# Second MLP product of a two-layer trunk: 12 of 16 pairs of k tiles computed with seven block products, their input sums made in the first product's stage

## The chip, the cores and the metric

The kernel runs on one core of a Trainium2 chip. A core has TensorE (PE, matmuls, whose weight loads the profile lists as PEld), VectorE (DVE), ScalarE (ACT), GpSimd (POOL) and SyncE (SP, which here only issues DMAs), each with its own queue of instructions, worked off in order. The metric is the device time of one execution, in microseconds. The kernel before took 3173.66 us (median of three runs, 3168.63 to 3181.02).

## What is computed

A trunk of two layers over 1024 tokens of width 1024. Layer 0 mixes tokens with two recurrent head groups, layer 1 with chunked attention. Every layer then has an MLP of inner width 4096 and a gated embedding. The reference, cut to what matters here:

```python
for i in range(DEPTH):
    ...
    x = x + mix
    hf = rmsnorm(x, norm_ffn_g[i])
    x = x + jnp.square(jax.nn.relu(hf @ mlp_w1[i])) @ mlp_w2[i]
    x = x + rmsnorm(p[i] @ ple_w_proj[i], ple_norm_g[i]) * jax.nn.sigmoid(x @ ple_w_gate[i])
return x
```

`mlp_w1[i]` is 1024 x 4096 and `mlp_w2[i]` 4096 x 1024, all in fp32.

## The kernel before

**Precision.** A product in fp32 is made of three matmuls in the format fp32r: each operand is split into a high part (a cast by ScalarE) and a low part (the operand minus the high part, by VectorE), and high x high, high x low and low x high are summed in PSUM (`mm3`). A matmul takes a 128x128 block of weights and 128x512 of activations (features on partitions, tokens along the row). `split` (L1264 to L1270) is the cast, L1269, and the subtraction, L1270.

**Stages.** `tail(i)` runs after the mixer of layer i, in one pass each for: the output projection (adds `mix` to the residual), the first MLP product, the second one, and the gate with the per-layer embedding. The residual has 8 tiles of 128 features; each is kept in two halves of 512 tokens (`self.xh`, `self.xh2`), in DRAM during the first product.

**First product, as seven block products.** The 32 output tiles are taken as 16 pairs, p = 0 to 15, and tokens in two halves, so that each round p is a 2x2 block problem over 8 input tiles in 4 pairs. In place of eight products of blocks, seven (numbered m, in the order 1, 2, 5, 6, 7, 3, 4) are made from sums and differences of blocks, each of 4 x 3 = 12 matmuls. The sums on the activation side (`cmb`) were made in the output projection. Those on the weight side, of the raw weights loaded by `raws(p)`, are made a round ahead by `prepare(p, m)` (L1337, L1341 and a split). A product lands in one of eight PSUM banks; the sums of products that give the four blocks of the output are made by VectorE in `plus` (L1371), into a ring of 8 quarter tiles (`scr`). `hidden` (L1374) applies relu and square on ScalarE and stores the block to DRAM (`self.hd`) on ScalarE's DMA queue, 256 KB each.

**Row statistics.** The norm's 1/rms of each token isn't known when the first product starts and is applied after it (squared, since relu and square come between). `squares(n)` loads residual tile n, squares it on ScalarE and adds it on VectorE (L1307 to L1315), one tile after each of the rounds p = 0 to 7, in the ring's tiles. After p = 8, `row_stats` sums over features with matmuls against ones, takes the inverse root in ten small vector operations in a row (L284 to L289, from the bank's copy at L373), and `to_rows` transposes the result with 8 small matmuls (L190) and copies it to `rs`; L1444 squares it.

**Second product.** `mlp2(g)` for g = 0 to 7 takes 4 of the 32 k tiles at a time. Their hidden tiles are loaded (L1397), multiplied by `rs` (L1401) and split during the group before; the weights come in 512 KB pieces (L1273) and are split, one piece ahead. For each of the 8 output tiles and both token halves 12 matmuls go into a bank, and VectorE adds the bank to the residual (L1470). After the last group the residual is split for the gate.

**What sets the order.** `tail` is a generator, run beside others that have work in the same stretch; within an engine the instructions stand in the order that a planner gives them from the dependencies and the program's order. Tiles come from pools: the pool of tag "a" has six places of 128 x 2 x 1024, in which weights and raw data take turns, so a tile's first write waits for the readers of the tile that had the place before. PSUM banks go round in the same way. All loads go through SyncE's queue in order, the hidden stores through ScalarE's.

Of the kernel before, what the change touches and what calls it, by code (L numbers as in the profile page):

```python
# [17 lines left out]
P = 128  # L18
# [8 lines left out]
PLAN_ROWS = 2  # L27

# [79 lines left out]
class Trunk:  # L108
# [56 lines left out]
    def mm(self, out, lhsT, rhs, start, stop):  # L165
# [9 lines left out]
        return self.begin(self.nc.tensor.matmul(out, lhsT, rhs, start=start, stop=stop))  # L175
# [129 lines left out]
    def mm3(self, ps, wh, wl, xh, xl, first, last):  # L305
        nc, steps = self.nc, self.steps
        ins = self.mm(ps, wh, xh, start=first, stop=False)
# [5 lines left out]
        self.mm(ps, wh, xl, start=False, stop=False)  # L313
        self.mm(ps, wl, xh, start=False, stop=last)
# [886 lines left out]
    def tail(self, i, xsrc):  # L1201
# [13 lines left out]
        with ExitStack() as es:  # L1215
# [46 lines left out]
            self.hd = [self.dr.tile([P, T], F32, tag=f"hd{k}", name="hd") for k in range(32)]  # L1262
# [106 lines left out]
            def plus(t, u):  # L1369
                r = scr()  # L1370
                V.tensor_tensor(r, t, u, op=ALU.add)  # L1371
                return r

            def hidden(t, k, hf):  # L1374
                A.activation(t, t, AF.Relu)
                A.activation(t, t, AF.Square)
                nc.scalar.dma_start(out=self.hd[k][:, hs[hf]], in_=t)

            H = [pB[0:4], None]

            w2 = {}

            rawb = []

            def raw_b():
                if not rawb:
                    rawb.extend(halves(place(F32)))
                return rawb.pop(0)

            def load_w2(n):  # L1390
                w2[n] = weights(a["w2"][i, n // 4, n % 4], raw_b(), place(F32R))

            hraw = {}

            def fetch_hidden(n, raw):
                hraw[n] = raw
                nc.sync.dma_start(out=raw, in_=self.hd[n])  # L1397

            def load_hidden(n):
                raw = hraw.pop(n)  # L1400
                V.tensor_tensor(raw, raw, rs, op=ALU.mult)  # L1401
                split(H[n // 4 % 2][n % 4], raw)

# [3 lines left out]
            for p in range(16):  # L1407
                k = 2 * p
# [589 lines left out]
```

## Time and profile before

| | |
|---|---|
| runs before | 3168.63, 3173.66, 3181.02 us |
| profiled execution, span from first to last instruction | 3174.0 us |
| mean granted clock of TensorE | 0.973 |
| busy: TensorE / VectorE / ScalarE / GpSimd | 96% / 64% / 44% / 17% |
| HBM read, written | 232.16 MB, 74.45 MB |
| tail of layer 0, by the chain of waits | 951.59 to about 1681 us |
| tail of layer 1 | 2370.99 us to the end |

A line of a timeline gives start, length, engine, line and operation, the tiles written and read, and in brackets how long the engine had been idle and what ended that. A line of groups gives the count, the busy time and the mean of one in ns, and the idle time ahead of such instructions. A line of the chain of waits gives start, length and what ran; "dps" is a PSUM bank. A matmul record is longer than the distance between two of them, since they overlap; the same holds for the vector and scalar records.

### The profile page before, as it was taken

What the parts mean: (1) busy time and instruction counts of PE and PEld (TensorE: products, weight loads), DVE (VectorE), ACT (ScalarE), POOL (GpSimd) and SP (SyncE); (2) the same over time, 40 slices, a digit from 0 to 9 for tenths busy, and PEclk for the clock granted to TensorE, in tenths of its full rate; (3) what the DMA queues carried; (4) which work ended last, traced back from release to release, by engine and by line L of the source; (5) the groups of instructions that cost most, each with busy time, mean ns of one, the idle gap of its engine ahead of it and who ended that gap; (6) DMA issues with size and microseconds to landing.
All of it is one profiled execution on the core that took longest, in us unless ns stands there. A gap on an engine that the chain in (4) does not pass through costs nothing.

```text
span 3174.0 us, 46034 instructions
## 1 busy us (share of the span) xinstructions
PE 3057.5 (96%) x17576; PEld 2523.9 (80%) x17576; DVE 2018.1 (64%) x4020; ACT 1387.8 (44%) x2640; POOL 536.1 (17%) x978
## 2 busy tenths in 40 slices
PE   7999999999999999999999989999999999999999
PEld 5777777777778888888887888888788888888887
DVE  6546666567849666655556576776769666655552
ACT  4323433333427554311223577777757555312221
POOL 6524443444500000000005111110200000000002
PEclk8989999999999999999999999999999999999999
DMA  3212112112345333522213100110255332522213
GB/s 128 77 48 64 50 43 85 54 57 64 126 153 209 136 120 112 190 93 100 99 54 129 58 32 33 47 39 16 76 197 205 136 120 107 199 93 93 107 47 106
DMA packets 144716, 309.60 MB, mean 98 GB/s; under 512 B 40944, under 2 KB 43120, under 8 KB 144496
## 3 DMA queue, kind: packets, MB, share of 16 engines
q1 hardware_dynamic: 126064, 273.10, 25.1%
q10 hardware_dynamic: 18432, 33.56, 2.7%
q8 instruction: 138, 2.26, 0.3%
q14 instruction: 82, 0.67, 0.1%
HBM read 232.16 MB, written 74.45 MB: 97 GB/s over the span
## 4 chain that ended last, share of the span: by engine, by line
PE 79%; DVE 10%; ACT 4%; DMA 4%; issue 2%; POOL 1%; SPq 0%; DVEq 0%; POOLq 0%; ACTq 0%
PE dps L175 67%; PE ch L175 2%; PE po L175 1%; PE pm L175 1%; PE iz L175 1%; PE tp L175 1%; DVE ptile L348 1%; PE pt L190 1%; DVE f L1056 1%; DMA wraw<-in_w_out 1%; PE sn L175 1%; DMA wraw<-in_w_qkv 1%; DVE wlo L302 1%; DVE pb L1838 1%; POOL subt L413 1%
## 5 line engine op out<-in xcount | busy, mean ns | idle before, releaser
L175 PE MATMUL dps<-r,act 128*128 128x512 f32 x3528 | 824.4, 392 | 0.0
L175 PEld LDWEIGHTS dps<-r,act 128*128 128x128 f32 x3528 | 662.2, 188 | 145.6
L175 PE MATMUL dps<-xg,whi 128*128 128x512 f32 x1280 | 437.9, 423 | 16.2 <-ACT xg L350 7.1
L175 PE MATMUL dps<-late,act 128*128 128x512 f32 x1536 | 352.9, 391 | 0.0
L175 PEld LDWEIGHTS dps<-late,act 128*128 128x128 f32 x1536 | 288.5, 188 | 63.1
L1495 POOL TENSOR_TENSOR pn<-pn,prs 128x512 f32<-128x512 f32 x32 | 47.1, 1475 | 1621.3 <-ACT prs L384 1527.3
L175 PE MATMUL dps<-wq,act 128*128 128x384 f32 x1536 | 304.8, 343 | 8.0 <-DVE vs L1747 4.2
L175 PEld LDWEIGHTS dps<-xg,whi 128*128 128x128 f32 x1280 | 237.2, 197 | 67.0 <-ACT xg L350 7.1
L175 PEld LDWEIGHTS dps<-wq,act 128*128 128x128 f32 x1536 | 264.5, 190 | 12.6 <-DVE vs L1747 7.0
L175 PE MATMUL dps<-xg,wlo 128*128 128x512 f32 x640 | 260.4, 408 | 2.0 <-DVE wlo L302 2.0
L1371 DVE TENSOR_TENSOR late<-late,dps 128x512 f32<-128x512 f32 x224 | 152.7, 684 | 152.4 <-PE dps L175 120.3
L1470 DVE TENSOR_TENSOR xw<-xw,dps 128x512 f32<-128x512 f32 x192 | 131.5, 685 | 154.6 <-PE dps L175 151.4
L1269 ACT CAST act<-act 128x1024 fp32r<-128x1024 f32 (+1 forms) x99 | 94.7, 963 | 282.9 <-DMA act<-in_w 119.4
L1269 ACT CAST act<-late 128x512 fp32r<-128x512 f32 x210 | 124.5, 618 | 139.5 <-PE dps L175 120.2
L1270 DVE TENSOR_TENSOR act<-late,act 128x512 fp32r<-128x512 f32 x210 | 139.7, 686 | 25.9 <-ACT act L1269 25.7
L175 PEld LDWEIGHTS dps<-xg,wlo 128*128 128x128 f32 x640 | 125.5, 196 | 33.2 <-DVE wlo L302 4.1
L301 ACT CAST whi<-wraw 128x1024 fp32r<-128x1024 f32 x78 | 81.7, 1048 | 152.7 <-PE dps L175 91.4
L175 PE MATMUL dps<-xw,act 128*128 128x512 f32 x576 | 138.9, 392 | 0.0
L175 PEld LDWEIGHTS dps<-xw,act 128*128 128x128 f32 x576 | 108.1, 188 | 24.1
L1270 DVE TENSOR_TENSOR act<-act 128x1024 fp32r<-128x1024 f32 (+1 forms) x99 | 109.9, 1114 | 18.3 <-ACT act L1269 17.2
L175 PE MATMUL po<-ptile,vs 128*128 128x256 f32 (+1 forms) x576 | 103.3, 293 | 17.5 <-DVE ptile L348 8.5
L302 DVE TENSOR_TENSOR wlo<-wraw,whi 128x1024 fp32r<-128x1024 f32 x78 | 99.3, 1274 | 27.5 <-ACT whi L301 27.1
(472 smaller groups left out, 5284.9 us busy)
## 6 DMA issues: line engine op xcount, KB each, us to landing
act<-in_w SPq DMA_DIRECT2D x68, 512.0 KB
hd<-late ACTq DMA_DIRECT2D x128, 256.0 KB
late<-in_w SPq DMA_DIRECT2D x60, 512.0 KB
wraw<-in_w_in SPq DMA_DIRECT2D x56, 512.0 KB
act<-hd SPq DMA_DIRECT2D x56, 512.0 KB
wraw<-in_w_out SPq DMA_DIRECT2D x21, 512.0 KB
wraw<-in_w_qkv SPq DMA_DIRECT2D x21, 512.0 KB
pn<-pnd SPq DMA_DIRECT2D x32, 256.0 KB
```

Source lines behind the costliest of these rows:

```text
L175: return self.begin(self.nc.tensor.matmul(out, lhsT, rhs, start=start, stop=stop))
L190: return self.begin(self.nc.tensor.transpose(out, in_, ident))
L301: nc.scalar.copy(hi, raw)
L302: nc.vector.tensor_tensor(lo, raw, hi.bitcast(F32), op=ALU.subtract)
L348: nc.vector.tensor_tensor(dst[:, 1, sl], src, dst[:, 0, sl].bitcast(F32), op=ALU.subtract)
L413: E.tensor_tensor(o, X[:, 0:i, i:i + 1].broadcast_to((NP, i, n)), Bq[:, i:i + 1, i + 1:16].broadcast_to((NP, i, n)), op=ALU.mult)
L1056: V.scalar_tensor_tensor(y, raws[j][:, i:i + HB], cw(i), y, op0=ALU.mult, op1=ALU.add)
L1269: A.copy(hi, s)
L1270: V.tensor_tensor(lo, s, hi.bitcast(F32), op=ALU.subtract)
L1371: V.tensor_tensor(r, t, u, op=ALU.add)
L1470: V.tensor_tensor(x[n][:, sl], x[n][:, sl], ps, op=ALU.add)
L1495: G.tensor_tensor(pn, pn, prs[:, sl], op=ALU.mult)
```

## The change

- The first 8 hidden tiles (the pairs p = 0 to 3, `PLAIN` = 4) are still stored as they are and multiplied plainly, in two groups of 4 k tiles: `plain(0)` at the start of the second product's stage and `plain(1)` at its end.
- The other 12 pairs are multiplied as 2x2 blocks with seven block products, four pairs at a time. In round n (0 to 11) the products of pairs n to n+3 (cyclic) are made for output pair n % 4; each round replaces one pair of the four, so that after three turns every output pair has seen all 12. A round is 7 products of 12 matmuls, in the order 1, 5, 6, 2, 7, 3, 4.
- Products 1, 6, 7, 4 add up in one PSUM bank without being cleared, 5 and 3 in another, 2 has its own. After each product VectorE adds the bank's present content to one block of the residual (`add_to`), and the next product of the chain goes on adding to it.
- The seven activation-side blocks are made in the first product's rounds p = 4 to 15 and stored to DRAM (`self.hb`, 7 x 256 KB a round in place of 4 x 256 KB): four scalings by `rs` and four differences on VectorE. For that, `rs` is needed from p = 4 on, so `squares` goes through three tiles after each of p = 0, 1, 2, with the single buffer "pl", and `row_stats` comes after p = 2.
- In the second product `block` loads and splits one stored block per product, and `raws2(n)` loads 4 x 256 KB of weights a round, of which `prepare2` makes and splits the weight side. `w2` is laid out anew by the host.
- `plus` writes in place where it can.

The diff, cut to its core:

```diff
+PLAIN = 4
+NB = 16 - PLAIN
...
-        return self.begin(self.nc.tensor.matmul(out, lhsT, rhs, start=start, stop=stop))
+        return self.begin(self.nc.tensor.matmul(out, lhsT, rhs, start=start, stop=stop, skip_group_check=again))
...
-            self.hd = [self.dr.tile([P, T], F32, tag=f"hd{k}", name="hd") for k in range(32)]
+            self.hd = [self.dr.tile([P, T], F32, tag=f"hd{k}", name="hd") for k in range(2 * PLAIN)]
+            self.hb = {p: self.dr.tile([P, 7, HB], F32, tag=f"hb{p}", name="hb") for p in range(PLAIN, 16)}
...
             def squares(n):
 
+                both = self.pre.tile([P, 2, HB], F32, tag="pl", name="xq")
                 for hf, src in ((0, self.xh[n]), (1, self.xh2[n])):
-                    t = scr()
+                    t = both[:, hf]
                     nc.sync.dma_start(out=t, in_=src)
                     if n:
...
-            def plus(t, u):
-                r = scr()
+            def plus(t, u, out=None):
+                r = out if out is not None else scr()
                 V.tensor_tensor(r, t, u, op=ALU.add)
                 return r
 
-            def hidden(t, k, hf):
+            def hidden(t, p, r, hf):
+
                 A.activation(t, t, AF.Relu)
                 A.activation(t, t, AF.Square)
-                nc.scalar.dma_start(out=self.hd[k][:, hs[hf]], in_=t)
-
...
+                if p < PLAIN:
+                    nc.scalar.dma_start(out=self.hd[2 * p + r][:, hs[hf]], in_=t)
+                else:
+                    V.tensor_tensor(t, t, rs[:, hs[hf]], op=ALU.mult)
+                    if (r, hf) != (0, 1):
+                        store(p, {(0, 0): 1, (1, 0): 2, (1, 1): 3}[r, hf], t)
+                return t
+
+            def store(p, m, t):
+                nc.scalar.dma_start(out=self.hb[p][:, m - 1], in_=t)
+
+            def differ(p, m, u, v, out=None):
+                t = out if out is not None else scr()
+                V.tensor_tensor(t, u, v, op=ALU.subtract)
+                store(p, m, t)
+                return t
...
+            def load_w2(g, u):
+                t, raw = place(F32R), self.pre.tile([P, 2, HB], F32, tag="pl", name="w2")
+                for j in range(2):
+                    nc.sync.dma_start(out=raw[:, j], in_=a["w2"][i, 2 * g + j, u])
+                split(t, raw.rearrange("p j c -> p (j c)"))
+                w2[g, u] = t[:, 0], t[:, 1]
...
+            def load_hidden(t, raw):
                 V.tensor_tensor(raw, raw, rs, op=ALU.mult)
-                split(H[n // 4 % 2][n % 4], raw)
+                split(t, raw)
...
+            def raws2(n):
+                t = place(F32)
+                for j in range(4):
+                    nc.sync.dma_start(out=t.rearrange("p q c -> p (q c)")[:, j * HB:j * HB + HB],
+                                      in_=a["w2"][i, PLAIN + (n + j) % NB, n % 4])
+                v = t.rearrange("p q c -> p (q c)").rearrange("p (j b c) -> p b j c", b=4, c=P)
+                prep2[n] = [v[:, b] for b in range(4)], {}
+
+            prep2, free2 = {}, []
+
+            def prepare2(n, m):
+
+                (a11, a12, a21, a22), d = prep2[n]
+                if not free2:
+                    free2.extend(parts(place(F32R)))
+                d[m] = free2.pop(0)
+                if m == 5:
+                    V.tensor_tensor(a21, a21, a22, op=ALU.add)
+                o, u, v = {1: (a11, None, None), 2: (a12, None, None), 5: (a21, None, None), 6: (a11, a21, a11),
+                           7: (a21, a22, a11), 3: (a12, a12, a11), 4: (a22, None, None)}[m]
+                if u is not None:
+                    V.tensor_tensor(o, u, v, op=ALU.subtract)
+                split(d[m], o)
+
+            def block(q, m):
+
+                raw = braw()
+                nc.sync.dma_start(out=raw, in_=self.hb[PLAIN + q % NB][:, m - 1])
+                split(areas[m][q % 4], raw)
...
                 if p < 15:
                     raws(p + 1)
                 else:
-                    for j in range(4):
-                        fetch_hidden(j, lt[2 + j // 2][:, j % 2])
-                    load_w2(0)
+                    load_w2(0, 0)
...
-                        hidden(plus(p1, ps), k, 0)
+                        c11 = hidden(plus(p1, ps), p, 0, 0)
                     elif m == 5:
                         p5 = ps
                     elif m == 6:
-                        u2 = plus(p1, ps)
+                        u2 = plus(p1, ps, p1)
                         u4 = plus(u2, p5)
                     elif m == 7:
-                        u3 = plus(u2, ps)
-                        hidden(plus(u3, p5), k + 1, 1)
+                        u3 = plus(u2, ps, u2)
+                        c22 = hidden(plus(u3, p5), p, 1, 1)
                     elif m == 3:
-                        hidden(plus(u4, ps), k, 1)
+                        c12 = hidden(plus(u4, ps, u4), p, 0, 1)
+                        if p >= PLAIN:
+                            differ(p, 7, c22, c12)
+                            t1 = differ(p, 5, c12, c11, c12)
+                            t2 = differ(p, 6, c22, t1)
                     else:
-                        hidden(plus(u3, ps), k + 1, 0)
+                        c21 = hidden(plus(u3, ps, u3), p, 1, 0)
+                        if p >= PLAIN:
+                            differ(p, 4, c21, t2)
                     if p < 15:
                         prepare(p + 1, prep_order[q])
+                    elif q == 1:
+                        hid = [fetch_hidden(0, k, h0[k], lt[2 + k // 2][:, k % 2]) for k in range(4)]
                     elif 2 <= q < 6:
-                        load_hidden(q - 2)
+                        load_hidden(*hid[q - 2])
                     yield 0
-                if p < NK:
-                    squares(p)
-                if p == NK:
+                if p < 3:
+                    for n in range(3 * p, min(3 * p + 3, NK)):
+                        squares(n)
+                if p == 2:
                     self.row_stats(accs, col)
...
+            areas[6], areas[2], areas[7], areas[3], areas[4] = pq[8:12], pq[12:16], cmb[4], pq[0:4], pq[4:8]
+            braw = ring([self.accp.tile([P, HB], F32, tag=f"acc{q}", name="braw") for q in range(2)] + quarters(place(F32)))
+            areas[1], areas[5] = [[c for q in qs for c in parts(place(F32R, True, f"r{q}"))] for qs in ((2, 3), (0, 1))]
...
+            def add_to(n, hf, ps):
+                V.tensor_tensor(x[n][:, hs[hf]], x[n][:, hs[hf]], ps, op=ALU.add)
...
+            def plain(g, hid, between):
+                for u in range(4):
+                    hi, lo = w2.pop((g, u))
+                    if u < 3:
+                        load_w2(g, u + 1)
                     for e in range(2):
+                        n = 2 * u + e
+                        for hf in range(2):
+                            ps = self.bank()
+                            for k in range(4):
+                                o = k // 2 * HB + e * 2 * P + k % 2 * P
+                                o = slice(o, o + P)
...
+            order2 = (1, 5, 6, 2, 7, 3, 4)
+            todo = [lambda q=q, m=m: block(q, m) for m in order2[:5] for q in range(4)]
+            todo2 = [lambda: raws2(0)] + [lambda m=m: prepare2(0, m) for m in order2]
+
+            def start_blocks(n, hf):
+                for _ in range(2 if n < 4 else 1):
+                    if todo:
+                        todo.pop(0)()
+                if n >= 4 and todo2:
+                    todo2.pop(0)()
+            yield from plain(0, h0, start_blocks)
+            for f in todo + todo2:
+                f()
+            for m in order2[5:]:
+                for q in range(4):
+                    block(q, m)
+            raws2(1)
+
+            chain = {1: 0, 5: 2, 6: 0, 2: 1, 7: 0, 3: 2, 4: 0}
+            goes = {1: (0, 0), 5: (1, 1), 6: (0, 1), 2: (0, 0), 7: (1, 1), 3: (0, 1), 4: (1, 0)}
+            for n in range(NB):
+                u, banks = n % 4, {}
+                for s, m in enumerate(order2):
+                    first = chain[m] not in banks
+                    if first:
+                        banks[chain[m]] = self.bank()
+                    ps, c = banks[chain[m]], prep2[n][1][m]
+                    for j in range(4):
+                        o, z = slice(j * P, j * P + P), areas[m][(n + j) % 4]
+                        self.mm3(ps, c[:, 0, o], c[:, 1, o], z[:, 0], z[:, 1], first and j == 0, j == 3, not first)
+                    e, hf = goes[m]
+                    add_to(2 * u + e, hf, ps)
+                    if n < NB - 1:
+                        block(n + 4, m)
+                        prepare2(n + 1, m)
+                        if s == 3 and n + 2 < NB:
+                            raws2(n + 2)
+                    elif s == 2:
+                        h1 = lates([F32R] * 4)
+                        raw = halves(place(F32)) + halves(place(F32))
+                        hid = [fetch_hidden(1, k, h1[k], raw[k]) for k in range(4)]
+                        load_w2(1, 0)
+                    elif s > 2:
+                        load_hidden(*hid[s - 3])
+                    yield 0
+            yield from plain(1, h1, lambda n, hf: self.split_scaled(xf[n], x[n][:, hs[hf]], None, hs[hf]))
...
-    out["w2"] = np.stack([w.reshape(8, 4, P, 4, 2, P).transpose(0, 3, 2, 4, 1, 5).reshape(8, 4, P, 1024)
+    out["w2"] = np.stack([w.reshape(16, 2, P, 4, 2, P).transpose(0, 3, 2, 4, 1, 5).reshape(16, 4, P, 512)
                           for w in f["mlp_w2"]])
```

More of the change, by code (lines that the diff above doesn't have):

```diff
@@ L163, in mark, with mm @@
         self.done[key] = self.now + after
-    def mm(self, out, lhsT, rhs, start, stop):
+    def mm(self, out, lhsT, rhs, start, stop, again=False):
         n, m = 1, 1
@@ L303, in split_w, with mm3 @@
         return hi, lo
-    def mm3(self, ps, wh, wl, xh, xl, first, last):
+    def mm3(self, ps, wh, wl, xh, xl, first, last, again=False):
         nc, steps = self.nc, self.steps
-        ins = self.mm(ps, wh, xh, start=first, stop=False)
+        ins = self.mm(ps, wh, xh, start=first, stop=False, again=again)
         while len(steps) > 1 and steps[1][0] <= self.now - LEAD:
@@ L312, in mm3 @@
                 mybir.DependencyClass.NoSync, mybir.DependencyReason.DATA), reason="order")
-        self.mm(ps, wh, xl, start=False, stop=False)
-        self.mm(ps, wl, xh, start=False, stop=last)
+        self.mm(ps, wh, xl, start=False, stop=False, again=again)
+        self.mm(ps, wl, xh, start=False, stop=last, again=again)
     def dense(self, w, acts, evac):
```

52 lines of the change are left out of this document (15 added, 37 removed).

## The prediction

> **What bounds the kernel now.** I began with the page: its busy times, then the 40 slices.
>
> ```profile
> span 3174.0 us, 46034 instructions
> ...
> PE 3057.5 (96%) x17576; PEld 2523.9 (80%) x17576; DVE 2018.1 (64%) x4020; ACT 1387.8 (44%) x2640; POOL 536.1 (17%) x978
> ...
> PE   7999999999999999999999989999999999999999
> ...
> PEclk8989999999999999999999999999999999999999
> ```
>
> TensorE is busy in every slice, at full clock almost everywhere, so the average says little more. The MLP is read in the chain of waits, in order of time (start, length, what). It runs along TensorE there without a break:
>
> ```profile
> 951.59 214.08 PE dps L175 x940
> ...
> 1166.55 481.04 PE dps L175 x2100
> 1648.46 32.66 PE dps L175 x143
> ...
> 2599.05 481.06 PE dps L175 x2100
> ```
>
> One matmul of 128x512 therefore sets the pace at 481.04/2100 = 0.2291 us; a product of 12 takes 2.75 us and a round of 84 takes 19.24 us. Whether other engines could ever stop it is seen in the windows (width, then busy time of PE, PEld, DVE, ACT, POOL, then clock, DMA share, GB/s): the first is the output projection, the second the second MLP product.
>
> ```profile
> 952.20:1031.50 79.30, 79.30 (x347) 64.94 (x346) 72.81 (x115) 57.56 (x100) 0.00 (x0) 1.00 0.60 209
> ...
> 1348.95:1428.30 79.35, 79.35 (x348) 65.14 (x347) 41.52 (x49) 13.55 (x14) 0.00 (x0) 1.00 0.27 93
> ```
>
> VectorE was 92% busy in the first and TensorE lost nothing; in the second it is half idle. The groups of instructions agree: matmuls of the first product never waited (the last column), while the vector sums wait for PE.
>
> ```profile
> L175 PE MATMUL dps<-late,act 128*128 128x512 f32 x1536 | 352.9, 391 | 0.0
> ...
> L1371 DVE TENSOR_TENSOR late<-late,dps 128x512 f32<-128x512 f32 x224 | 152.7, 684 | 152.4 <-PE dps L175 120.3
> L1470 DVE TENSOR_TENSOR xw<-xw,dps 128x512 f32<-128x512 f32 x192 | 131.5, 685 | 154.6 <-PE dps L175 151.4
> ```
>
> **What is removed.** The second product has 32 x 8 x 2 x 3 = 1536 matmuls per layer. After the change 8 k tiles stay plain (384) and 12 rounds of 7 x 4 x 3 = 84 make 1008: 1392. That is 144 fewer per layer, 288 in all, and 288 x 0.2291 = **66.0 us**, all on the path.
>
> **Vector and scalar work.** Durations overlap, so I price by pitch (start to start): VectorE 0.60 us for 128x512 and 1.13 for 128x1024, ScalarE 0.52, a store's issue on ScalarE's queue 0.33.
>
> ```profile
> 959.73 0.69 DVE L1303 TENSOR_TENSOR act<-act 128x512 f32<-128x512 f32 x1
> 960.33 0.68 DVE L1296 TENSOR_TENSOR act<-act,dps 128x512 f32<-128x512 f32 x1
> ```
>
> ```profile
> 1346.09 1.22 DVE L1270 TENSOR_TENSOR act<-act 128x1024 fp32r<-128x1024 f32 x1
> 1347.22 1.22 DVE L1270 TENSOR_TENSOR r<-act,r 128x1024 fp32r<-128x1024 f32 x1
> ```
>
> ```profile
> 1196.86 0.62 ACT L1269 CAST act<-late 128x512 fp32r<-128x512 f32 x1
> 1196.92 0.33 ACTq L1377 DMA_DIRECT2D hd<-late  x1
> 1197.38 0.62 ACT L1269 CAST act<-late 128x512 fp32r<-128x512 f32 x1
> ```
>
> In the first product a round with p ≥ 4 gets 4 scalings and 4 differences: 26 vector operations instead of 18, 26 x 0.60 = 15.6 us of 19.24; ScalarE has 16 operations and 7 stores, 16 x 0.62 + 7 x 0.33 = 12.2. Weights are prepared a round ahead, which hides it: I take 0. Were that cover gone, a round could lose no more than a few tenths (the 92% window above lost none).
>
> In the block rounds VectorE does 7 sums into the residual, 7 + 7 splits and 4 weight sums: 25 x 0.60 = 15.0 us of 19.24; ScalarE's 14 casts take 14 x 0.62 = 8.7. A sum waits for its product, and behind it in VectorE's queue stand the next block's and weights' splits, for which TensorE waits. The handover is new: products 1, 6, 7, 4 share an accumulator and 5, 3 another, each read by VectorE before the next may add. A bare handover costs about 0.87 us (the read of the last rows below starts 0.09 us after PE's end and takes 0.69; as much again for the restart). In the built program's order 23 to 28 other matmuls (5.3 to 6.4 us) stand between such a read and the next use. I take 0; bounds 0 and 4 x 0.87 x 24 rounds = 84 us. Following the prices through a round, the tightest weights (those whose buffer comes free with product 4 of the round before) are ready 2 to 3 us ahead, an estimate.
>
> **Row statistics, moved from after p = 8 to after p = 2.** Before, 24 matmuls stood between the statistics and their transposes and covered VectorE's serial chain (timelines of PE, then of DVE):
>
> ```profile
> 1158.22 1.84 PE L175 MATMUL dps<-ones,acc 128*128 128x1 f32 x16
> 1159.92 5.76 PE L175 MATMUL dps<-r,act 128*128 128x512 f32 x24
> 1165.51 1.04 PE L190 MATMUL dps<-ident,col 128*128 128x128 f32 x8
> ```
>
> ```profile
> 1160.22 0.15 DVE L373 TENSOR_SCALAR ms<-dps 128x8 f32<-128x8 f32 x1
> ...
> 1162.71 0.17 DVE L289 SCALAR_TENSOR_TENSOR col<-rsw,col 128x8 f32<-128x8 f32 x1
> ...
> 1165.77 0.69 DVE L1371 TENSOR_TENSOR late<-late,dps 128x512 f32<-128x512 f32 x1 [2.90 <-PE dps L175]
> ```
>
> That chain is 2.66 us. In the built program's order the transposes stand directly behind the statistics, so nothing covers it. Worse is what precedes them: eight k tiles of squares pass through one buffer, three per round instead of one, each load behind the sums of the tile before. SyncE issues six such loads a round between the weights' loads. One load takes 2.7 us from issue to use:
>
> ```profile
> 1073.73 0.33 SPq L1311 DMA_DIRECT2D late<-xh  x1
> ```
>
> ```profile
> 1076.41 0.63 ACT L1313 ACTIVATE late<-late 128x512 f32<-128x512 f32 x1 [0.21 <-DMA late<-xh]
> ```
>
> By the order, tile 6's sums end about when TensorE runs out of work (layer 0 has two more products, but starts tile 6 later). The last tile then costs 0.4 for the issue, 2.7 to land, 0.63 to square, 0.6 to add = 4.3; statistics 0.9 (8 of the 16 matmuls' time); the chain 2.7; transposes 0.5: about **8.5 us** of idle TensorE per layer. Bounds: 3 (the chain alone) and 13 (a tile more).
>
> A long idle also costs clock. The one wait of over 5 us late in the trace shows it (PE timeline, then windows):
>
> ```profile
> 1748.50 1.86 PE L175 MATMUL dps<-ones,acc 128*128 128x1 f32 x8 [5.34 <-POOL acc L1508]
> 1751.13 9.04 PE L175 MATMUL dps<-wq,act 128*128 128x384 f32 x39 [0.76 <-DVE ms L373]
> ```
>
> ```profile
> 1748.50:1751.00 2.50, 1.86 (x8) 1.78 (x8) 2.45 (x3) 1.04 (x1) 1.76 (x4) 0.50 0.10 29
> 1751.00:1754.00 3.00, 2.87 (x9) 2.88 (x10) 1.43 (x8) 0.75 (x1) 1.77 (x3) 0.50 0.85 284
> 1754.00:1757.00 3.00, 3.00 (x16) 3.00 (x15) 1.75 (x5) 1.02 (x3) 0.00 (x0) 0.79 0.28 76
> ```
>
> The clock is 0.50 to 1754 and 0.79 on average in the next 3 us, so half until about 1755.3: 4.1 us at half speed from 1751.13, 2.1 us of work lost. With this **2 x (8.5 + 2.1) = 21 us**.
>
> [...]
>
> **The two seams of the second product.** Loads of 512 KB took 3.6 us to their use:
>
> ```profile
> 1348.47 0.32 SPq L1397 DMA_DIRECT2D act<-hd  x1
> ```
>
> ```profile
> 1352.09 1.22 DVE L1401 TENSOR_TENSOR act<-act,rs 128x1024 f32<-128x1024 f32 x1 [0.43 <-DMA act<-hd]
> ```
>
> At the start of the block rounds the second round's 1 MB of weights are issued 27 matmuls (6.2 us) ahead with block loads before them; at 1 MB I put 5.7 to 7.7 us, so 1.5 us late per layer: **3 us** (0 to 8). At the last plain group the four hidden tiles are issued 12 matmuls (2.7 us) before VectorE wants the first, 2 MB and the weights behind one another, and each needs 1.13 us to scale and 1.13 to split: about 4 us per layer, **8 us** (0 to 20; the upper end with two losses of clock). VectorE's queue waits there with the sums of products 7, 3, 4 behind.
>
> In round p = 15 VectorE has 15 x 0.60 and 9 x 1.13 us = 19.2 against TensorE's 19.24: the first plain group starts up to 2 us late, **3 us** in both layers (0 to 5). That plain group also loads ahead the blocks, while the residual's loads arrive; the queues were full at this point before and TensorE did not notice:
>
> ```profile
> 1290.00:1300.00 10.00, 10.00 (x46) 8.15 (x45) 3.44 (x5) 3.79 (x6) 0.00 (x0) 1.00 1.04 370
> ```
>
> Block rounds move 7 x 256 KB and 1 MB, 2.88 MB per 19.24 us or 150 GB/s, and 11 issues on SyncE; 0.
>
> **Sum.** 3174.0 - 66.0 + 21 + 3 + 8 + 3 = **3143 us** against the profiled execution. That execution lies 0.3 us above the median of the runs, so nothing is added.
>
> **Rivals.** *A, the whole gain.* The squares are early enough and the seams are covered: 3174 - 66 + 2 x 3.5 for the bare chain = 3115, and 3108 if that too is hidden. For it: the window in which VectorE is 92% busy and TensorE full. Against it: the single buffer and the transposes' place.
>
> *B, the handovers show.* VectorE's sums fall behind, and two of a round's four handovers are bare: 3143 + 2 x 0.87 x 24 = 3185, no change. Against it: 23 matmuls of cover. For it: a sum queued behind a split that waits, as in the next row.
>
> *C, conversions become the bound of the block rounds (slower).* A vector split waits for ScalarE's cast where the order brings the two too close:
>
> ```profile
> 1188.99 0.69 DVE L1270 TENSOR_TENSOR act<-late,act 128x512 fp32r<-128x512 f32 x1 [1.06 <-ACT act L1269]
> ```
>
> With k such waits a round lasts 15.0 + 1.06k us, and this passes 19.24 at k = 4. Then weights come late each round. With k = 7 (one kind of split always exposed) it is 22.4 us: 24 x 3.2 = 77, 3143 + 77 = 3220. It is slower by 0.5% from 21.2 us a round, k = 6. Against it: in the output projection 115 vector operations ran in 79.3 us at 92%, with the same two engines alternating.
>
> **How the numbers follow.** The forecast gets 0.54, A 0.18, B 0.15, C 0.13. Its own range, by the terms' bounds, is 3117 to 3169 (the terms do not all reach their ends together). To leave out 2 in 10, the range runs from 3108 (A with everything hidden) to 3174: above it lie C and part of B. A measurement here tells 0.5% (16 us) from no change: below 3158 is faster. Nearly all of the forecast's chance and all of A's lie there, 0.72; B with a little of the forecast gives 0.15 for no change; C, 0.13 for slower.
>
> **What would show it.** Right: 17288 matmuls in all; rounds of 84 matmuls in 19.24 us in the block stage with no idle of TensorE; one idle of about 8 us in each layer a few products after p = 2, ended by the add of squares and then by the statistics' vector chain, with a clock of 0.5 behind it; idles of some us at the last plain group, ended by hidden loads. Wrong: rounds over 19.5 us with waits for sums (B) or for splits (C), or no idle at the statistics (A).

## The result, and the profile after

| | median of runs | profiled span |
|---|---|---|
| before | 3176.0 us (3168.6 to 3181.0, 4 runs) | 3174.0 us |
| after | 3130.6 us (3126.4 to 3138.5, 4 runs) | 3128.3 us |

The ratio is 0.9859, with a 95% interval of 0.9836 to 0.9883. The forecast was 3143 us, a gain of 31 us; the measured gain is 45.4 us. The page of the changed kernel, in the lines shown of before:

```profile
span 3128.3 us, 47113 instructions
...
PE 3000.5 (96%) x17288; PEld 2476.6 (79%) x17288; DVE 2234.1 (71%) x4518; ACT 1510.6 (48%) x2922; POOL 532.5 (17%) x978
...
PE   7999999999999999999999898999899999999999
...
PEclk8989999999999999999999999999999999999999
```

There are 17288 matmuls, 288 fewer, as worked out. HBM traffic rose to 262.04 MB read and 93.32 MB written. The 40 slices of 78 us don't show where time was lost: the 8s lie at 1720, 1877 and 2190 us, outside both tails, and an idle of 7 us still leaves a 9. The chain of waits shows it: in each tail TensorE's chain breaks at one place, before 1059 us in layer 0 and before 2463 us in layer 1, and everything behind it is unbroken again:

```profile
967.19 65.99 PE dps L177 x286
1059.42 565.96 PE dps L177 x2460
...
2463.36 571.01 PE dps L177 x2484
```

571.01/2484 is 0.2299 us per matmul, with the slow first ones in it, against 0.2291 before. The figure of before holds for the block rounds too, with VectorE at 81% (a window over nearly eleven of layer 0's rounds; columns as before):

```profile
1350.28:1560.85 210.57, 210.57 (x920) 172.58 (x919) 171.34 (x277) 90.24 (x154) 0.00 (x0) 1.00 0.49 154
```

210.57/920 = 0.2289 us, so 84 matmuls take 19.2 us: TensorE lost nothing there. Of its waits in the whole run (engine, tile, what ended them, total, times, longest), these are the two largest new rows:

```profile
PE dps L192 <- DVE col L291: 6.1, 2, 3.9
...
PE dps L177 <- DVE acc L1318: 5.6, 3, 3.1
```

Both belong to the row statistics. Layer 0, on PE, then VectorE, then SyncE:

```profile
1045.37 1.52 PE L177 MATMUL dps<-x,act 128*128 128x512 f32 x6
1050.03 3.57 PE L177 MATMUL dps<-ones,acc 128*128 128x1 f32 x16 [3.14 <-DVE acc L1318]
1057.45 1.97 PE L192 MATMUL dps<-ident,col 128*128 128x128 f32 x8 [3.85 <-DVE col L291]
1059.07 3.34 PE L177 MATMUL dps<-r,act 128*128 128x512 f32 x7
```

```profile
1055.45 0.17 DVE L290 SCALAR_TENSOR_TENSOR rsw<-rsw,ms 128x8 f32<-128x8 f32 x1
1056.63 0.69 DVE L1341 TENSOR_TENSOR late<-late 128x512 f32<-128x512 f32 x1 [1.01 <-DMA late<-in_w]
1057.24 0.16 DVE L291 SCALAR_TENSOR_TENSOR col<-rsw,col 128x8 f32<-128x8 f32 x1
```

```profile
1045.10 0.32 SPq L1315 DMA_DIRECT2D xq<-xh  x1
...
1051.20 0.81 SPq L1405 DMA_DIRECT2D w<-in_w  x2
1052.11 0.38 SPq L1327 DMA_DIRECT2D late<-in_w  x1
```

The last squares are loaded at 1045.10, 1.8 us before TensorE runs out of work. Then comes the vector chain, and in it a piece that has nothing to do with the statistics: the last of its ten operations stands behind a sum of weights (L1341), whose load waits in SyncE's queue behind the second product's first weights (L1405), which became issuable when the squares' buffer came free. That makes the chain 3.8 us; by itself it is 2.2 us, as in layer 1 (the 2.66 us read in the kernel before had a split in it). The windows there show the clock:

```profile
1050.00:1052.00 2.00, 1.97 (x10) 1.97 (x10) 1.87 (x3) 0.71 (x2) 0.00 (x0) 0.50 0.00 0
...
1060.00:1065.00 5.00, 5.00 (x16) 3.90 (x15) 1.23 (x1) 0.63 (x2) 0.00 (x0) 0.65 0.00 0
```

It is at 0.50 from the end of the first idle on (0.99 on average in 1045 to 1050 us), so the statistics took 3.57 us where they took 1.84 before, the transposes 1.97 where they took 1.04, and the first matmuls after them run at half speed (seven in 3.34 us in PE's last row, where six take 1.52 in its first).

### The profile page after: what moved, and what is told of

It reads as the page before. It is cut to its first block, busy times and chain, and to the rows that moved or that the text cites. A ratio compares the mean times of both kernels' runs of the same rounds, so it can differ in the third digit from the quotient of the medians.

```text
span 3128.3 us, 47113 instructions
## 1 busy us (share of the span) xinstructions
PE 3000.5 (96%) x17288; PEld 2476.6 (79%) x17288; DVE 2234.1 (71%) x4518; ACT 1510.6 (48%) x2922; POOL 532.5 (17%) x978
## 3 DMA queue, kind: packets, MB, share of 16 engines
q1 hardware_dynamic: 158608, 303.00, 29.9%
HBM read 262.04 MB, written 93.32 MB: 114 GB/s over the span
## 4 chain that ended last, share of the span: by engine, by line
PE 79%; DVE 10%; ACT 4%; DMA 3%; issue 2%; POOL 1%; SPq 0%; DVEq 0%; ACTq 0%; POOLq 0%
PE dps L177 67%; PE ch L177 2%; PE pm L177 1%; PE po L177 1%; PE tp L177 1%; PE iz L177 1%; DVE ptile L350 1%; PE pt L192 1%; DVE f L1058 1%; PE sn L177 1%; PE py L177 1%; DVE pb L1942 1%; ACT pb L1955 1%; DVE wlo L304 1%; POOL subt L415 1%
## 5 line engine op out<-in xcount | busy, mean ns | idle before, releaser
L177 PE MATMUL dps<-late,act 128*128 128x512 f32 x960 | 229.3, 392 | 0.0
L177 PEld LDWEIGHTS dps<-late,act 128*128 128x128 f32 x960 | 180.3, 188 | 39.7
L1272 ACT CAST act<-act 128x512 fp32r<-128x512 f32 (+1 forms) x223 | 137.7, 648 | 129.5 <-PE dps L177 67.4
L1272 ACT CAST act<-late 128x512 fp32r<-128x512 f32 x210 | 124.3, 618 | 136.2 <-PE dps L177 89.3
L177 PE MATMUL dps<-act 128*128 128x512 f32 x672 | 165.2, 392 | 0.0
L1273 DVE TENSOR_TENSOR act<-act 128x512 fp32r<-128x512 f32 (+1 forms) x223 | 155.0, 722 | 5.9 <-ACT act L1272 5.7
L1273 DVE TENSOR_TENSOR act<-late,act 128x512 fp32r<-128x512 f32 x210 | 141.3, 687 | 11.2 <-ACT act L1272 9.3
L177 PEld LDWEIGHTS dps<-act 128*128 128x128 f32 x672 | 126.2, 188 | 28.7
L1507 DVE TENSOR_TENSOR xw<-xw,dps 128x512 f32<-128x512 f32 x174 | 118.0, 683 | 32.4 <-PE dps L177 32.2
L1380 ACT ACTIVATE late<-late 128x512 f32<-128x512 f32 x128 | 80.2, 629 | 118.4 <-DVE late L1375 112.0
```

The lines of the kernel that those rows point to most:

```text
L1272: A.copy(hi, s)
L1273: V.tensor_tensor(lo, s, hi.bitcast(F32), op=ALU.subtract)
L1507: V.tensor_tensor(x[n][:, hs[hf]], x[n][:, hs[hf]], ps, op=ALU.add)
```

## Where the gain went

The tail of a layer can be measured from the output projection's first matmul to the transposes of the gate's norm (`prsc`). PE's timeline has these two rows for layer 0, before and after:

```profile
951.59 0.73 PE L175 MATMUL dps<-xg,wh 128*128 128x512 f32 x2 [0.32 <-DVE act L1296]
...
1647.42 1.04 PE L190 MATMUL dps<-ident,prsc 128*128 128x128 f32 x8
```

```profile
949.24 0.73 PE L177 MATMUL dps<-xg,wh 128*128 128x512 f32 x2 [0.32 <-DVE act L1299]
...
1625.23 1.03 PE L192 MATMUL dps<-ident,prsc 128*128 128x128 f32 x8
```

Layer 0 took 695.83 us before and 675.99 after; layer 1, read in the same way, 696.47 and 672.00. The removed matmuls are worth 33.0 us each, so 13.2 and 8.5 us were given back, 21.7 in all. The experiments ask whether that is the statistics alone, and why the three other terms (14 us) didn't come.

## The experiments

All medians beside the median of the kernel before on the same chip. An edit is against the changed kernel unless it says "on top of e1".

**e1: statistics after p = 3.**

```diff
-                if p == 2:
+                if p == 3:
                     self.row_stats(accs, col)
```

> Row statistics called after p = 3 instead of p = 2, squares left where they are: the last squares are then done a round ahead, and in the built order 24 matmuls stand again between the statistics and their transposes. Theory: all that the change lost against the 66 us of removed matmuls (about 21 us: TensorE idle 11.7 us at the statistics, the half clock behind it) comes from this place, so the span falls from 3128 to about 3107 to 3110, a ratio to the kernel before near 0.979, with no wait of TensorE for acc or col left. Rival 1, the loss is spread over the rounds (denser VectorE and DMA work slows TensorE): less than 10 us gained, span 3118 or more. Rival 2, the wait moves to p = 4, whose scalings need rs: no gain, and VectorE waits for rs with TensorE behind it.

Measured: 3110.3 us against 3176.6, ratio 0.9789 (0.9771 to 0.9808); profiled span 3105.5. No wait of TensorE for `acc` or `col` is left. PE's timeline in layer 0:

```profile
1059.07 1.84 PE L177 MATMUL dps<-ones,acc 128*128 128x1 f32 x16
1060.78 1.65 PE L177 MATMUL dps<-xw,act 128*128 128x512 f32 x6
1062.26 1.54 PE L177 MATMUL dps<-x,act 128*128 128x512 f32 x6
1063.64 2.93 PE L177 MATMUL dps<-r,act 128*128 128x512 f32 x12
1066.41 1.04 PE L192 MATMUL dps<-ident,col 128*128 128x128 f32 x8
```

The 24 matmuls are back between the statistics and their transposes, and these two take 1.84 and 1.04 us again, as in the kernel before (3.57 and 1.97 in the changed kernel); the mean granted clock of the profiled run is 0.974, against 0.968. The tails take 663.27 and 663.67 us: 12.7 and 8.3 us less than in the changed kernel, **21.0 us** together, and 32.6 and 32.8 us less than before. That is practically the whole 66 us. Both rivals fall, and this version, with one digit changed, beats both kernels.

**Which part of the statistics costs: e2, e3, e11, e13.** e2 takes the squares into the old ring:

```diff
-                both = self.pre.tile([P, 2, HB], F32, tag="pl", name="xq")
...
-                    t = both[:, hf]
+                    t = scr()
```

> Squares loaded into the ring of eight quarter tiles as before instead of the one buffer, statistics still after p = 2. Theory: the wait for the last squares (5.6 us in both layers) goes, the wait for the serial vector chain at the transposes (2.3 us or more per layer) stays; each idle is then short enough that the clock hardly falls, so 3128 falls to about 3113 to 3118. Rival, the ring's tiles are scarce (its sums of products now wait for squares): TensorE waits elsewhere, 3125 or more.

Measured: 3130.6 us, 0.9852 (0.9836 to 0.9869), as the changed kernel. The waits for squares fell only from 5.6 to 4.6 us. The theory missed: the last squares were issued at 1042.85 us, only 2 us earlier. Places in the ring are scarce, as the rival had it: between 1000 and 1060 us SyncE's loads of squares waited 16.2 us for the sums of earlier squares and 9.2 us for stores of hidden tiles. But TensorE did not wait elsewhere for it. Nor did the shorter idles save the clock: behind one of 2.51 us in layer 0 it was 0.84 on average from 1045 to 1050 us and 0.50 from there to 1054.

e3 moves only the transposes and `rs`:

```diff
                 if p == 2:
                     self.row_stats(accs, col)
-                    self.to_rows(col, rs)
-                    V.tensor_tensor(rs, rs, rs, op=ALU.mult)
...
+                    if (p, q) == (3, 3):
+                        self.to_rows(col, rs)
+                        V.tensor_tensor(rs, rs, rs, op=ALU.mult)
```

> Statistics after p = 2 as in the change, only the transposes and rs later, after four products of p = 3, squares still in the one buffer. Theory: the waits at the transposes (6.1 us in both layers) go; of the wait for the last squares less or nothing stays since products of p = 3 stand in front of the statistics too; span about 3107 to 3116. Rival, the wait for squares is what costs, and it stays: 3120 or more.

Measured: 3120.8 us, 0.9817 (0.9795 to 0.9839). In layer 1 no wait is left; in layer 0 the statistics stand in another place and TensorE waits 8.6 us for the squares. So both parts cost, and the squares' lateness isn't cured by what is done behind them.

e11 calls the squares earlier, e13 lets each half of the buffer go by itself:

```diff
-                if p < 3:
-                    for n in range(3 * p, min(3 * p + 3, NK)):
+                if p < 2:
+                    for n in range(4 * p, 4 * p + 4):
                         squares(n)
```

> The change itself, statistics after p = 2, squares through the one buffer but four tiles after each of p = 0 and 1, so that none is left for p = 2. In the built order the transposes still stand directly behind the statistics. Theory: the wait for the last squares (5.6 us in both layers) goes, the wait for the vector chain (about 2.7 us per layer) stays, too short for the clock to fall: 3128 falls to 3110 to 3118 (e1 plus 5 us for the chains). Rival: the clock falls all the same, or squares of rounds 0 and 1 hold TensorE up: 3120 or more.

```diff
+            xq = []
             def squares(n):
-                both = self.pre.tile([P, 2, HB], F32, tag="pl", name="xq")
+                if not n:
+                    xq.append(self.pre.tile([P, 2, HB], F32, tag="pl", name="xq"))
                 for hf, src in ((0, self.xh[n]), (1, self.xh2[n])):
-                    t = both[:, hf]
+                    t = xq[0][:, hf]
```

> The change itself, statistics after p = 2, squares in the one buffer but taken once for all eight tiles, so that each half is loaded again as soon as its own sum is done instead of when both halves' are. In e11's trace the eight tiles follow each other at 6.5 us whatever the round they are called in, so the buffer's pace is what makes them late. Theory: with the halves free by themselves (their sums are 1.2 to 1.8 us apart) a tile takes about 5 us, the last sums are done some 10 us earlier and the wait of TensorE for them (5.6 us in both layers) goes; the chain's wait (2.3 us or more per layer) stays: 3110 to 3120. Rival: the pace is set by ScalarE's and VectorE's queues, in which squares stand behind other work, and stays: 3125 or more.

e11 measured 3132.3 us, 0.9865 (0.9849 to 0.9880): nothing gained. SyncE's timeline tells why (first and last of the eight tiles):

```profile
1000.35 0.33 SPq L1315 DMA_DIRECT2D xq<-xh  x1
...
1045.57 0.32 SPq L1315 DMA_DIRECT2D xq<-xh  x1
```

The last tile goes out at 1045.57, where the changed kernel had 1045.10, though it was called a round earlier. Seven steps take 45.2 us, 6.5 us each: the pace of one buffer through load, square and sum decides, not the round in which a tile is called. e13 measured 3117.3 us, 0.9813 (0.9790 to 0.9835), and in neither layer is there a wait for `acc`:

```profile
1048.73 1.52 PE L177 MATMUL dps<-x,act 128*128 128x512 f32 x6
1050.09 1.84 PE L177 MATMUL dps<-ones,acc 128*128 128x1 f32 x16
1055.07 1.97 PE L192 MATMUL dps<-ident,col 128*128 128x128 f32 x8 [3.14 <-DVE col L291]
```

```profile
1052.00:1054.00 2.00, 0.00 (x0) 0.00 (x0) 1.86 (x8) 0.62 (x1) 0.00 (x0) 0.88 0.11 40
1054.00:1056.00 2.00, 0.93 (x5) 0.94 (x6) 0.84 (x6) 0.00 (x0) 0.00 (x0) 0.50 0.62 193
```

Its tiles follow each other at 5.4 us (37.6 us for seven steps on SyncE). What remains against e1 is the bare chain: the tails are 669.48 and 668.63 us, 6.2 and 5.0 us longer, of which 3.1 and 3.5 us are idle. Here too the clock fell to a half, at about 1053.5 us, 1.6 us into the idle that began at 1051.9 (0.88 on average from 1052 to 1054, 0.50 to 1058), against what I expected in e2 and e11; the last section sets these idles side by side.

**The handovers: e6, e8, e9 (on top of e1).** e6 orders the products 5, 1, 6, 7, 4, 2, 3:

```diff
-                for s, m in enumerate(order2):
+                for s, m in enumerate((5, 1, 6, 7, 4, 2, 3)):
```

> On top of e1: in the block rounds the products in the order 5, 1, 6, 7, 4, 2, 3, so that in the built order mostly 9 to 14 other matmuls (2.1 to 3.2 us) stand between a product and the next one in its bank, where 23 to 28 stood. Theory (a bare handover costs about 0.9 us and VectorE's queue adds little): the cover is still enough, time as e1 within 5 us. Rival B of the prediction (VectorE's sums line up behind splits): waits of TensorE for the sums into x appear, at 1 to 2 us each and two to three in a round 25 to 100 us more than e1.

Measured: 3137.8 us, 0.9867 (0.9846 to 0.9889), 27.5 us more than e1. But no wait is one for a sum. In layer 0 they are these, in layer 1 nearly the same:

```profile
PE dps L177 <- DVE act L1273: 8.1, 4, 2.9
PE dps L177 <- ACT act L1272: 1.0, 1, 1.0
```

L1273 is a split, L1272 its cast. Neither theory expected this: the accumulators keep up, while the splits have less slack in this order, in which the same loop also loads and splits the next blocks and weights. These waits are 17.6 us in both layers; the rest of the 27.5 and which split is late were not followed further.

e8 keeps the order and ties each product behind the end of the one before in TensorE's order (`after` adds that edge in `mm3`); e9 exchanges products 5 and 1 in addition, so that product 6 follows 1 in its bank at once.

```diff
-                        self.mm3(ps, c[:, 0, o], c[:, 1, o], z[:, 0], z[:, 1], first and j == 0, j == 3, not first)
+                        end = self.mm3(ps, c[:, 0, o], c[:, 1, o], z[:, 0], z[:, 1], first and j == 0, j == 3, not first, end)
```

```diff
-                for s, m in enumerate(order2):
+                for s, m in enumerate((5, 1, 6, 2, 7, 3, 4)):
```

> On top of e1: in the block rounds TensorE must take the products in the program's order 1, 5, 6, 2, 7, 3, 4, each to its end, so 12 other matmuls (2.75 us) stand between products of the first chain where 23 to 28 stood. Theory (a handover takes about 0.9 us, VectorE's sums come soon after): no wait of TensorE for sums into x, time as e1 within 5 us. Rival B of the prediction (sums lined up behind splits for more than 2 us): such waits appear, three a round, 50 us or more in all. A third outcome is waits for splits of weights, as in e6, since product 4 at the round's end is what sets their buffer free: 10 to 50 us.

> As e8, with products 5 and 1 exchanged: product 6 follows product 1 in the same bank with nothing between, once a round in 24 rounds; the other handovers keep 12 matmuls. This measures the bare handover by itself. Theory: 0.9 us each, so 24 x 0.9 = 21 us more than e8 (15 to 30), shown as about 24 waits of TensorE for VectorE's sum into x. If VectorE's queue delays the sum: 2 us each, 50 us more. If TensorE need not wait for the read: 0.

e8 measured 3114.6 us, 0.9802 (0.9771 to 0.9833), which can't be told from e1. TensorE waits for a sum once in each layer (1.5 and 1.4 us); everywhere else 12 matmuls of cover (2.75 us) are enough. e9 measured 3161.8 us, 0.9953 (0.9935 to 0.9972), 47 us more than e8. PE's timeline, two of its rounds:

```profile
1393.04 5.75 PE L177 MATMUL dps<-r,act 128*128 128x512 f32 x24 [0.87 <-DVE xw L1510]
...
1414.14 5.75 PE L177 MATMUL dps<-r,act 128*128 128x512 f32 x24 [1.57 <-DVE x L1510]
...
1434.54 5.75 PE L177 MATMUL dps<-r,act 128*128 128x512 f32 x24 [0.87 <-DVE xw L1510]
```

The shortest wait is the 0.87 us of the prediction. But the sum is often behind another operation in VectorE's queue: 20 such waits in both layers total 29.9 us, 1.5 us each (the waits of layer 0, and of layer 1: 14.4 and 15.5 us), and waits for splits and casts add 7 us. Part of the other 10 us is the clock, 0.96 and 0.98 in two windows of 79 us of layer 0 where e8 has 1.00. These two rounds last 21.1 and 20.4 us instead of 19.2. So a handover left bare in every round costs about 2 us a round with all that follows from it, more than twice the price I had put; the cover is what made it nothing.

**VectorE's room: e4, e5 (on top of e1).** The subtraction of a split is done twice, in e4 for the stored blocks, in e5 for the weights also.

```diff
-            def split(c, s):
+            def split(c, s, times=1):
...
-                V.tensor_tensor(lo, s, hi.bitcast(F32), op=ALU.subtract)
+                for _ in range(times):
+                    V.tensor_tensor(lo, s, hi.bitcast(F32), op=ALU.subtract)
...
-                split(areas[m][q % 4], raw)
+                split(areas[m][q % 4], raw, 2)
```

> On top of e1: the low part of each stored block is made twice (same result), 32 instead of 25 vector operations a round, 32 x 0.60 = 19.2 us against TensorE's 19.24. Theory: VectorE is almost at the bound, with some of its waits exposed: 0 to 40 us more than e1. If VectorE's rounds already had no room (rival C of the prediction), 24 x 4.2 = 100 us more.

> On top of e1: the low parts of blocks and of weights are made twice, 39 vector operations a round, 39 x 0.60 = 23.4 us. Theory: VectorE is now the bound, each of 24 rounds takes 23.4 us plus the waits it can't hide: 24 x 4.2 = 100 us more than e1 or above, with TensorE waiting for splits in every round and VectorE over 95% busy. If less than 60 us, the price of 0.60 us for an operation is too high here.

e4 measured 3129.0 us, 0.9850 (0.9822 to 0.9879), 19 us over e1; e5 3227.7 us, 1.0151 (1.0119 to 1.0183), 117 us over e1. The same window of layer 0 in e4, then in e5:

```profile
1419.00:1498.00 79.00, 78.51 (x340) 63.04 (x339) 78.45 (x132) 32.42 (x56) 0.00 (x0) 1.00 0.48 147
```

```profile
1419.00:1498.00 79.00, 70.09 (x279) 54.23 (x278) 78.02 (x130) 27.20 (x47) 0.00 (x0) 0.94 0.42 124
```

VectorE is full in both, at 0.59 to 0.60 us an operation (78.45/132, 78.02/130). At 32 operations a round TensorE still does 340 matmuls in 79 us, where the full pace is 345; at 39 it does 279. The pitch of 0.60 us prices it: 24 x (23.4 - 19.2) = 100 us of the 117, and the clock's fall (0.94 in this window) is part of the rest. Of e4's 19 us, 8.6 are one wait for a sum in each layer (4.4 and 4.2 us). So VectorE's bound lies at about 32 operations a round, and the change has 25. C's own mechanism, splits that wait for ScalarE's casts, was not produced by itself in any run.

**The last seam: e10, e12 (on top of e1).** The first of the four hidden tiles of the last plain group, or all four, are loaded twice.

```diff
-                nc.sync.dma_start(out=raw, in_=self.hd[4 * g + k])
+                for _ in range(1 + (g == 1 and k == 0)):
+                    nc.sync.dma_start(out=raw, in_=self.hd[4 * g + k])
```

> On top of e1: at the last plain group the first of the four hidden tiles is loaded twice into the same place, the second load behind the first, so that it and those behind it land about 3.3 us later. In e1's trace the split tiles were ready 3 to 4 us before TensorE took them. Theory (VectorE's lateness at the seam was absorbed by about 35 matmuls that TensorE still had): 0 to 3 us more than e1, no wait of TensorE over 1 us per layer. Rival (there is no such reserve, as the prediction had it): 3.3 us per layer and a fall of the clock, 7 us or more.

> As e10, with all four hidden tiles loaded twice, so each is later by one more load: 3.3, 6.6, 10 and 13 us. Theory: the reserve of 3 to 4 us is used up and TensorE waits in each layer, 5 to 10 us, with waits for the splits of hidden tiles: 10 to 25 us more than e1 with the clock's share. If it is still 0, the reserve is far larger than read.

Measured: e10 3111.3 us, 0.9803 (0.9782 to 0.9824); e12 3107.7 us, 0.9785 (0.9768 to 0.9803). Neither differs from e1, and TensorE has no wait over 0.2 us there. For e12 that is more reserve than I had read. But TensorE's order changed in both: behind the 48 matmuls on `r` at this seam in layer 0, e1 has 19 on `late`, then 12 on `act`; e10 and e12 have 4 on `late` and then the 12. So the tests moved work as well as loads, and the reserve itself isn't measured.

## Why the prediction was right, point by point

- **What is removed, 66.0 us:** right. e1 is 66.3 us below the kernel before (3176.6 - 3110.3), and its two tails are 65.4 us shorter. (The row of 1536 matmuls from which the prediction read that the first product never waits belongs to the second product, its matmuls starting at 1339.8 us. The rows of the first product have no idle time either.)
- **Vector and scalar work, 0:** right, for the reason given. A pitch of 0.60 us is confirmed by e4 and e5, the handover's cover by e8. What I had wrong is the bare price, 0.87 us where e9 shows 1.5 us of wait.
- **Row statistics, 21 us:** right in place and in size, 21.0 us measured by e1, but the size is luck. The idle was 7.0 us in layer 0 (3.14 + 3.85) and 4.8 in layer 1, 11.8 us together where 17 were priced. Of each 8.5 us, 1.4 were the statistics' and transposes' own matmuls, which the kernel before ran too. That leaves about 9 us for the half clock, where 4.2 were priced: it fell earlier than behind the last idle, in layer 0 ahead of the statistics, in layer 1 ahead of the transposes, so that these ran at half speed too (3.57 us for the statistics in layer 0, 1.97 for the transposes in both, where the kernel before took 1.84 and 1.04). The last squares took 6.1 us from their issue (1045.10) to the last sum's end (1051.2), not 4.3: the load took 3.5 us to its square and not 2.7, and the second half's sum stood behind a sum of weights (L1345), as ScalarE's and VectorE's timelines show. And the chain of layer 0 had another sum of weights in it. These errors offset each other.

```profile
1048.62 0.63 ACT L1317 ACTIVATE xq<-xq 128x512 f32<-128x512 f32 x1 [1.07 <-DMA xq<-xh]
```

```profile
1049.89 0.69 DVE L1345 TENSOR_TENSOR late<-late 128x512 f32<-128x512 f32 x1
1050.49 0.68 DVE L1318 TENSOR_TENSOR acc<-acc,xq 128x512 f32<-128x512 f32 x1
```

- **The seams, 3 + 8 + 3 us:** wrong, all three were 0: behind the output projection neither tail has a wait of TensorE besides those at the statistics. These 14 us are what the forecast gain fell short of the measured one. The lateness I had worked out was there, but it was VectorE's. On SyncE, VectorE and PE, at the last plain group of layer 0 in the changed kernel:

```profile
1563.62 6.36 SPq L1410 DMA_DIRECT2D act<-hd  x4
```

```profile
1567.34 1.23 DVE L1414 TENSOR_TENSOR act<-act,rs 128x1024 f32<-128x1024 f32 x1 [1.69 <-DMA act<-hd]
...
1570.81 1.22 DVE L1273 TENSOR_TENSOR late<-act,late 128x1024 fp32r<-128x1024 f32 x1
```

```profile
1575.74 4.51 PE L177 MATMUL dps<-late,act 128*128 128x512 f32 x19
```

VectorE waited 1.69 us for the first tile, which landed 3.7 us after its issue, as priced. The split that follows (L1273, into `late`) ended at 1572.0, and TensorE's next matmuls on `late` start at 1575.74, having had block products to do until then. I set the load's issue against VectorE's use and charged the difference to TensorE. The same holds for the second round's weights, where VectorE waited 1.53 us and TensorE not at all:

```profile
1359.89 0.69 DVE L1437 TENSOR_TENSOR act<-act 128x512 f32<-128x512 f32 x1 [1.53 <-DMA act<-in_w]
```

- **The rivals:** A's 3115 or 3108 was not what the change did, but e1 comes to it, at 3110.3: A's conditions hold once the statistics come a round later. B and C did not happen. e9 shows that B's mechanism is real, at 47 us, beyond the cover that the change has. e5 shows that a full VectorE costs 117 us, though it was filled by doubled subtractions and not by C's waits for casts.

## What to carry to other kernels

A wait is charged to the engine that sets the end only after asking what that engine still has to do; an issue compared with the next engine's use gives that engine's wait, not the end's. When a serial piece (loads through one buffer, a chain of small operations) is moved earlier, what covered it doesn't move with it: count the buffer's pace from its first tile to its last, and look at what stands in the order between the piece and its use. Where the cover depends on the order, one round later can be worth as much as a third of a large saving (21 of 66 us here).

## What the runs showed of the hardware

- Idles of TensorE of 2.1 to 3.5 us in the middle of a full load were followed by half clock in the cases that follow. In layer 0 of e11 an idle of 3.02 us ended at 1050.39, and the statistics behind it took 3.58 us, where the kernel before took 1.84. In layer 0 of e2 one of 2.51 us ended at 1047.07 (granted clock 1.00 from 1040 to 1045 us, then 0.84 and 0.50 as above); in layer 1, behind a wait of 2.1 us, the statistics took 3.48 us by the chain of waits, from 2454.54 on. In layer 1 of e13 one of 3.47 us ended at 2453.38 (1.00 from 2450 to 2452, 0.74 on average to 2454, 0.50 to 2456). In layer 1 of the changed kernel the small matmuls of the statistics stand between two idles of 2.3 us, and the clock fell at about 2459.6, early in the second (PE's timeline, then windows):

```profile
2456.86 1.05 PE L177 MATMUL dps<-ones,acc 128*128 128x1 f32 x8 [2.35 <-DVE acc L1318]
2458.07 1.05 PE L177 MATMUL dps<-ones,acc 128*128 128x1 f32 x8 [0.15 <-DVE acc L1318]
2461.39 1.97 PE L192 MATMUL dps<-ident,col 128*128 128x128 f32 x8 [2.27 <-DVE col L291]
```

```profile
2458.00:2460.00 2.00, 1.05 (x8) 0.97 (x8) 1.86 (x8) 1.31 (x3) 0.00 (x0) 0.89 0.40 123
2460.00:2462.00 2.00, 0.61 (x3) 0.61 (x4) 1.13 (x7) 0.00 (x0) 0.00 (x0) 0.50 0.78 299
```

- Not every such idle cost the clock, and it did not fall at the same point of each. Through the 2.35 us ahead of the statistics in these rows, and to 2459.5, it stayed at 1.00. Where it fell within an idle (an estimate from the average clock of the window with the fall, as one change from 1.00 to 0.50), it did so 3.0 us after the idle's start in layer 0 of the changed kernel (at 1049.86; 0.86 from 1049.5 to 1050), 0.4 us in layer 1 (at 2459.56; 0.56 from 2459.5 to 2460), and 1.6 and about 3 us in the two layers of e13. What decides this is not shown by these runs; the shortest of these idles, 2.1 us, was not safe.
- Half clock lasted longer than the idles. By the same estimate the clock of the changed kernel was full again at 1063.51 us in layer 0 (0.50 from 1063 to 1063.5, 0.99 in the next 0.5 us) and at 2466.39 in layer 1 (0.61 from 2466 to 2466.5): 13.7 and 6.8 us after its fall, and 6.1 and 5.0 us after TensorE's last idle there had ended (at 1057.45 and 2461.39).
